# A macaron layer on one core: the recurrence's gates in two groups, the value products behind the transposes, the last sum of squares in its own tile

## The chip, the cores and the metric

The kernel runs on one core of one Trainium2 chip. The core's engines run side by side and each takes its own instructions in order: TensorE (PE, with its weight loader PEld), VectorE (DVE), ScalarE (ACT), GpSimd (POOL), and SyncE (SP), which issues transfers; ACT and POOL issue some too. An instruction that waits holds all that is queued behind it on its engine. The time of a kernel is the device time of one execution in microseconds (us).

## The reference

One layer, 512 tokens of width 1024 in float32: a half-step SwiGLU feed-forward (2816 wide), a mixer, and a second half-step feed-forward. Each is normed before and behind, and added to the stream.

```python
def hybrid_mixer(h, ...):
    proj = h @ w_in                     # x_lru, gate_lru, q, k, v
    y_lru = rg_lru(x_lru, ...) * jax.nn.gelu(gate_lru)
    y_attn = sliding_window_sink_attention(q, k, v, sinks)
    y = jnp.concatenate([rms_norm(y_lru, g_lru_out), rms_norm(y_attn, g_attn_out)], axis=-1)
    return y @ w_o

def rg_lru(x_in, ...):                  # 512 channels
    xc = causal_depthwise_conv(x_in, conv_w, conv_b)
    r = sigmoid(block_diag(xc, w_rg, b_rg))      # 8 blocks of 64x64
    i = sigmoid(block_diag(xc, w_ig, b_ig))
    log_a = LRU_C * r * log_sigmoid(lam)
    u = sqrt(-expm1(2.0 * log_a)) * (i * xc)
    return scan of h = exp(log_a) * h + u
```

The attention has 8 query heads of 64 in two groups, each group with one key and value head, windows of 128 tokens (a query block of 128 looks at its own block of keys and the one before), and a sink in the softmax. The very last step is the root mean square norm of the second feed-forward's output and the addition to the stream:

```python
def rms_norm(x, g):
    y = x * rsqrt(mean(x * x, axis=-1) + 1e-6)
    return y * g
```

## The kernel before, in words

All large products are made from two parts of each number: x = xh + xl, where `xh` is rounded to the short form (fp32r) that PE multiplies fast and `xl` is the rest. `mm3` (lines 500 to 507) issues hi·xh, hi·xl, lo·xh; these are the lines L505, L506 and L507 of every timeline. ACT makes the high part by a cast and POOL or DVE the low part by a subtraction. Weights are split likewise as they arrive (`whi_...` on ACT, `wlo_...` on DVE or POOL).

The order of the work is written out by hand: each engine works in the order in which the program calls it.

The mixer's stretch around the change goes so. The inner channels and tokens lie with the channels on the partitions: 512 channels are four chunks of 128 channels by 512 tokens. PE makes the products of k (`pk`), v (`pv`) and the four chunks of q (`pq0` to `pq3`), some 24 matmuls of 0.23 us each. Beside them DVE makes the causal convolution of chunks 0 and 1, and then of 2 and 3 (`conv`, L1442 to L1446), and scales each product from PSUM as it comes (`scaled`, L1426). `in_parts` (L1483 to L1493) does this for k and q, copies the first block to `home` and splits the rest in two parts.

`split_xc(ci)` (L1472, L1473) splits the convolution's output: the cast on ACT, the subtraction on POOL. `lru_gates(ci)` makes the two gates of a chunk: six matmuls with 64 rows each, the two halves of the partitions side by side (L1454), two sigmoids on ACT (L1456, L1458), two transfers on SP which bring the halves of both gates to where they belong (L1457, L1459), the multiplication of the input gate with the channels on POOL (L1461), and a third transfer which POOL issues (L1462). It is called for chunk j behind `pq`j. Behind `pq0` and its gates v is transposed (`vt`, L1512). SP also loads the weights of the mixer's output (`raw_wo`, L174), between these transfers.

The first query block has only its own keys; its scores (`cur`, L1610) are sixteen small products of 64 rows straight from `home`, for head 0 to head 3, and need all four chunks of q. They stand behind `pq3` and its gates.

Then come the attention's rounds (the loop over `now`). A unit is a query block and a group of heads, 8 units in all. In round `now` the scores of unit `now` are masked and their maxima taken on DVE, the exponentials are made on ACT (`exps`, L1652); unit `now`−1 is transposed on PE (`turn_p`, `pt`, L1664), copied out by ACT (L1666) and masked by POOL into `pp` and `pa` (L1670, L1671); and unit `now`−2 is multiplied with v (`values`, `po`, L1683 and L1684). Transposes and value products use plain float32. Between them `pump(n)` issues n steps of the gate's product (`gt`), each of three matmuls, so that PE has work. `PUMPS` gives how many go ahead of the transposes, and how many between them and the value products. In round 5 and 6 the recurrence's square roots stand on ACT (`root`, with two table loads).

The tail makes the last feed-forward's output in blocks of 128 tokens; the last block (`tb` = 3) comes in three pieces of 512, 256 and 256 columns. For each piece DVE takes the product out of PSUM (L1983), ACT squares and sums it (L1984) and DVE multiplies it with the gain (L1988). When all three sums are there, they are added on DVE (L1986, L1990), ACT takes the root (L1995), DVE the reciprocal (L1996), and three DVE operations multiply and add the stream (L1999); three transfers write them out (L2000).

Of the kernel before, what the change touches and what calls it, by code (L numbers as in the profile page):

```python
# [8 lines left out]
F32 = mybir.dt.float32  # L9
F32R = mybir.dt.float32r  # L10
U8 = mybir.dt.uint8
AF = mybir.ActivationFunctionType
ALU = mybir.AluOpType
AX = mybir.AxisListType

P = 128
T = 512
NB = T // P
D = 1024
# [4 lines left out]
KC = C // P  # L24
HD = 64
EPS = 1e-6
# [4 lines left out]
NWS = 6  # L31
NRAW = 5
CLASSIC1, CLASSIC2 = 4, 6
PUMPS = [(2, 1)] * 8 + [(1, 1), (1, 0), (4, 0)]
FILLS = {1: 4, 2: 5, 4: 5, 5: 5, 7: 5}
WARM = 6
AHEAD = 4
# [84 lines left out]
def tile_layer(ctx: ExitStack, tc: tile.TileContext, out: bass.AP, **ins: bass.AP):  # L122
    nc = tc.nc
    pe, dve, act, pool, sync = nc.tensor, nc.vector, nc.scalar, nc.gpsimd, nc.sync
# [5 lines left out]
    small = ctx.enter_context(tc.tile_pool(name="small", bufs=4))  # L130
# [8 lines left out]
    SIDE = [slice(0, HD), slice(HD, P)]  # L139

    def bank(name):
        return psum.tile([P, T], F32, tag="bank", name=name)

    def t2k(name, dt=F32):
        return big.tile([P, T], dt, tag="t2k", name=name, bufs=NT2K)
# [3 lines left out]
    def fours(name, dt):  # L149
        t = big.tile([P, NB * T], dt, tag="z", name=name, bufs=2)  # L150
        return [t[:, i * T:(i + 1) * T] for i in range(NB)]
# [10 lines left out]
    def wt(name, w=T, dt=F32):  # L162
        return tmp.tile([P, w], dt, tag="w", name=name, bufs=NW)
# [23 lines left out]
    class Shared:  # L187


        parts = slice(0, KD // 2), slice(KD // 2, KD)  # L190
# [259 lines left out]
    for name, n in ROWS:  # L450
        if name in ("b_rg", "b_ig"):

            j = name == "b_ig"
# [14 lines left out]
    def filled(name, w, value):  # L468
        t = const.tile([P, w], F32, name=name)
        dve.memset(t, value)  # L470
        return t
# [5 lines left out]
    eps4 = filled("eps4", 1, 4 * EPS)  # L477
    dummy = const.tile([P, 1], F32, name="dummy")

    def preload(func):  # L480
        act.activation(dummy, eps, func)
# [9 lines left out]
    def col(name, i):  # L491
        return colrange(name)[:, i:i + 1]
# [16 lines left out]
    def product(w, xs, sl=ALL, name="", hooks=()):  # L509
        ps = bank(name)  # L510
        hooks = dict(hooks)
        for k, x in enumerate(xs):
            if k in hooks:
                hooks[k]()
            mm3(ps[:, sl], w, k, [t[:, sl] for t in x], k == 0, k == len(xs) - 1)
        return ps
# [683 lines left out]
    banks = [bank(f"a_first{i}") for i in range(4)]  # L1200
# [96 lines left out]
    gw, home = {}, []  # L1297
# [60 lines left out]
    parts = [None] * KD  # L1358
# [63 lines left out]
    def in_product(name, hooks=(), ahead=AHEAD):  # L1422
        return product(W.take(ahead), mx.xs, name=name, hooks=hooks)

    def scaled(t, b):
        dve.tensor_mul(t, b, R)  # L1426
        return t
# [17 lines left out]
                ci = c0 + j  # L1445
                dve.scalar_tensor_tensor(xcs[ci], xps[ci][:, 1 + w:1 + w + T], col("conv_w", w * KC + ci), xcs[ci], op0=ALU.mult, op1=ALU.add)  # L1446

    def lru_gates(ci):

        banks = bank(f"rg{ci}"), bank(f"ig{ci}")  # L1450
        (hi, lo), (xh, xl) = gw["both"], xc_parts[ci]
        for i, (w, x) in enumerate(((hi, xh), (hi, xl), (lo, xh))):
            for ps, half in zip(banks, SIDE):
                pe.matmul(ps, w[half, ci, :], x[half, :], start=i == 0, stop=i == 2)  # L1454
        r, other, ig = t2k(f"r{ci}"), wt(f"other{ci}"), wt(f"ig{ci}")
        act.activation(r, banks[0], AF.Sigmoid, bias=col("b_rg", ci))  # L1456
        sync.dma_start(ig[SIDE[0], :], r[SIDE[1], :])  # L1457
        act.activation(other, banks[1], AF.Sigmoid, bias=col("b_ig", ci))  # L1458
        sync.dma_start(ig[SIDE[1], :], other[SIDE[0], :])  # L1459
        u = xcs[ci]  # L1460
        pool.tensor_mul(u, ig, u)  # L1461
        pool.dma_start(r[SIDE[1], :], other[SIDE[1], :])  # L1462
        t = t2k(f"th{ci}")
        rs_.append(r)
        us_.append(u)
        th.append(t)

    xc_parts = {}

    def split_xc(ci):  # L1470
        xh, xl = wt(f"xch{ci}", T, F32R), wt(f"xcl{ci}", T, F32R)
        act.copy(xh, xcs[ci])  # L1472
        pool.tensor_sub(xl, xcs[ci], xh.bitcast(F32))  # L1473
        xc_parts[ci] = xh, xl
# [8 lines left out]
    def in_parts(b, first, name, low=dve):  # L1483

        x = scaled(wt(name), b)
        dve.tensor_copy(first, x[:, :P])
        if name == "qT3":
            spare.extend(fours("attn", F32R))
            xh, xl = spare.pop(), spare.pop()
        else:  # L1490
            xh, xl = t2k(f"{name}h", F32R), t2k(f"{name}l", F32R)
        act.copy(xh, x)
        low.tensor_sub(xl, x, xh.bitcast(F32))  # L1493
        return xh, xl

    conv(0, xps)
    split_xc(0)
    kT = in_parts(pk, k0, "kT", pool)
    pv = in_product("pv")
    vT = scaled(wt("vT"), pv)  # L1500
    conv(2, xps)
    qT = []
    for j in range(4):
        b = in_product(f"pq{j}")
        if j < KC - 1:
            split_xc(j + 1)
        lru_gates(j)
        qT.append(in_parts(b, q0[:, j * P:(j + 1) * P], f"qT{j}", deferred if j == 3 else dve))
        if j == 0:
            vt = bank("vt")  # L1510
            for b in range(NB):
                pe.transpose(vt[:, b * P:(b + 1) * P], vT[:, b * P:(b + 1) * P], ident)  # L1512
            v = home[0][:, 3 * T:]
            dve.tensor_copy(v, vt)
# [50 lines left out]
    now = 0  # L1565
    steps = fill_steps()

    def pump(n):
        for _ in range(n):
            next(steps, None)  # L1570
# [12 lines left out]
    def root(ci):  # L1583
        act.activation(th[ci], th[ci], AF.Sqrt)
# [10 lines left out]
    scale = HD ** -0.5  # L1595
# [121 lines left out]
    for now in range(n_units + 2):  # L1717
        if now < n_units:
            scores(*units[now])
            if now in FILLS:  # L1720
                W.fill(FILLS[now])
        pump(PUMPS[now][0])
        if 0 <= now - 1 < n_units:
            turn_p(*units[now - 1])
        if now < n_units:
            exps(*units[now])
        if now == 0:
            deferred.run()
        if now <= n_units:
            run_due(now - 1)  # L1730
        pump(PUMPS[now][1])
        if 0 <= now - 2:
            values(*units[now - 2])
        if now == 5:
            for ci in range(KC):
                root(ci)
            preload(AF.Exp)
        if now == 6:
            for ci in range(KC):
                root_u(ci)  # L1740
            for ci in (2, 3):
                scan(ci)
        if now == n_units:
            scan(0)
            deferred.run()
            preload(AF.Sqrt)
            root_rms(slice(0, NB - 1))
# [62 lines left out]
    ws, banks = [], []  # L1810
    for c in range(EARLY):
# [9 lines left out]
        if c == EARLY - 2:  # L1821
            bcs = [l.spread() for l in lrms]
            for ci in range(KC):
                for h in range(2):
                    dve.tensor_mul(hl[ci][:, HALF[h]], hl[ci][:, HALF[h]], bcs[h])
                y = t2k(f"ylh{ci}", F32R), t2k(f"yll{ci}", F32R)
# [15 lines left out]
    banks = boundary(res, late, ysp, None, n2, "m")  # L1842
# [23 lines left out]
    parts = {(tb, dh): hbm.tile([P, T], F32, name=f"yp_b{tb}{dh}") for tb in range(NB) for dh in range(2)}  # L1866
# [43 lines left out]
    grow = []  # L1910

    def read_gain():
        for dh in range(2):
# [3 lines left out]
    last = {-1: [lambda: (read(0, 0), read(0, 1), read(1, 0), read(1, 1), read_gain(), read_x(0))],  # L1917
            2: [lambda: hid.fetched(f0, h_hbm[f0])], 3: [lambda: read_x(1)], 4: [lambda: (hid.split(f0), hid.split(f0 + 1))]}
# [42 lines left out]
    pieces = {tb: [(0, 0, T)] + ([(1, 0, T // 2), (1, T // 2, T)] if tb == NB - 1 else [(1, 0, T)]) for tb in range(NB)}  # L1961
# [13 lines left out]
    for tb in range(NB):  # L1975
        end = tb == NB - 1
        last = []
        ss = small.tile([P, 3], F32, tag="ss3", name=f"ss_b{tb}")
        tot = small.tile([P, 1], F32, tag="tot", name=f"tot_b{tb}")
        for i, (dh, c0, c1) in enumerate(pieces[tb]):  # L1980
            out_products(tb, i, range(f0 + 2 * ((tb, i) in started), f1))
            y = parts[tb, dh][:, c0:c1]
            dve.scalar_tensor_tensor(y, place(tb, i), -1.0 if dh else 1.0, y, op0=ALU.mult, op1=ALU.subtract if dh else ALU.add)  # L1983
            act.activation(wt(f"ysq{tb}{i}")[:, :c1 - c0], y, AF.Square, accum_out=ss[:, i:i + 1])  # L1984
            if end and i == 2:
                dve.tensor_add(tot, ss[:, 0:1], ss[:, 1:2])  # L1986
            last.append(wt(f"last{tb}{i}")[:, :c1 - c0])
            (dve if end or i else pool).tensor_mul(last[i], y, grow[dh][:, c0:c1])  # L1988
        if end:
            dve.tensor_add(tot, tot, ss[:, 2:3])  # L1990
        else:
            dve.tensor_add(tot, ss[:, 0:1], ss[:, 1:2])

        rs = small.tile([P, 1], F32, tag="rs1", name=f"rs_b{tb}")
        act.activation(rs, tot, AF.Sqrt, bias=eps4, scale=4.0 / D)  # L1995
        dve.reciprocal(rs, rs)  # L1996
        for i, (dh, c0, c1) in enumerate(pieces[tb]):
            y = parts[tb, dh][:, c0:c1]
            dve.scalar_tensor_tensor(y, last[i], rs, x_rows[tb][:, dh * T + c0:dh * T + c1], op0=ALU.mult, op1=ALU.add)  # L1999
            (act if end and i == 1 else sync).dma_start(out[0, tb * P:(tb + 1) * P, dh * T + c0:dh * T + c1], y)  # L2000
# [28 lines left out]
```

## Time and profile before

| | us |
|---|---|
| median of 3 runs | 845.67 (845.57 to 845.91) |
| span of the profiled execution | 843.6 |
| PE busy | 834.5 (99%) |
| DVE busy | 732.7 (87%) |
| ACT busy | 523.8 (62%) |
| POOL busy | 201.7 (24%) |

The profiled execution took 843.6 us from its first to its last instruction; what lies around that span is in the median and not in the profile. The mean granted clock of TensorE is 0.998.

A row of a timeline gives the start, the duration, the engine, the line, the operation, the tiles (out<-in), their shape, how many instructions stand in the row, and in brackets the idle time ahead of it on its engine with what ended it. Matmuls overlap in the pipeline: the distance between the starts of two is what one costs, not the duration. A row of the waits gives an engine's line and what it waited for: the sum in us, how often, and the longest.

### The profile page before, as it was taken

How to read it: one execution, taken by the hardware profiler on the slowest of the kernel's cores; microseconds unless marked ns; L12 is line 12 of the kernel's file. 1: busy time of each engine (PE TensorE's matmuls, PEld its weight loads, DVE VectorE, ACT ScalarE, POOL GpSimd, SP SyncE). 2: the span in 40 equal slices, each digit the busy share in tenths (PEclk: the TensorE clock that was granted, in tenths of full speed). 3: DMA queues.
4: the chain of work that ended last, by engine and by line, in shares of the span. 5: the costliest groups of instructions: out<-in, count | busy, mean ns of one | idle time of the engine just before them, and what ended most of it. 6: DMA issues, size and time to landing. Idle time of an engine off the chain costs nothing.

```text
span 843.6 us, 12618 instructions
## 1 busy us (share of the span) xinstructions
PE 834.5 (99%) x4568; PEld 722.6 (86%) x4568; DVE 732.7 (87%) x1020; ACT 523.8 (62%) x874; POOL 201.7 (24%) x214
## 2 busy tenths in 40 slices
PE   9999999999999999999999999999999999999996
PEld 8988888988988998997788899888888888888885
DVE  4978999998979865889899589799998998998996
ACT  6646856666666655456788457436757767666552
POOL 2023000140320333334646055112004113032001
PEclk9999999999999999999999999999999999999999
DMA  7249419397595799222511131169539939769742
GB/s 251 77 131 348 151 59 322 80 254 254 129 248 185 169 261 343 77 79 91 158 50 51 50 110 42 50 137 273 186 108 231 322 91 249 249 154 262 295 137 101
DMA packets 123615, 143.75 MB, mean 170 GB/s; under 512 B 23896, under 2 KB 81568, under 8 KB 123040
## 3 DMA queue, kind: packets, MB, share of 16 engines
q1 hardware_dynamic: 109232, 111.86, 41.6%
q0 software_dynamic: 14176, 30.94, 17.0%
q8 instruction: 36, 0.59, 0.3%
q14 instruction: 27, 0.22, 0.1%
q10 hardware_dynamic: 144, 0.13, 0.0%
HBM read 100.45 MB, written 40.89 MB: 168 GB/s over the span
## 4 chain that ended last, share of the span: by engine, by line
PE 97%; ACT 1%; DVE 1%; DMA 1%; issue 0%; POOL 0%; DVEq 0%; POOLq 0%; ACTq 0%
PE ab L955 10%; PE aa L955 10%; PE da L955 5%; PE db L955 5%; PE yaa L1345 3%; PE bb L955 3%; PE ba L955 3%; PE yda L1345 2%; PE ya L507 2%; PE ya L505 2%; PE ya L506 2%; PE a_first L1205 1%; PE aa L885 1%; PE yab L1875 1%; PE yab L1874 1%; PE yab L1876 1%
## 5 line engine op out<-in xcount | busy, mean ns | idle before, releaser
L1115 POOL DMA_DIRECT2D yp_a<-stage x42 | 36.9, 1085 | 181.2 <-ACT stage L1112 160.9
L1115 POOL DMA_DIRECT2D yp_b<-stage x42 | 36.4, 1091 | 144.6 <-ACT stage L1112 121.1
L505 PE MATMUL ya<-hha,whi_ad 128*128 128x512 f32 x62 | 24.1, 389 | 0.0
L506 PE MATMUL ya<-hla,whi_ad 128*128 128x512 f32 x62 | 24.1, 389 | 0.0
L507 PE MATMUL ya<-hha,wlo_ad 128*128 128x512 f32 x62 | 24.1, 389 | 0.0
L688 POOL TENSOR_TENSOR acca_r<-acca_r,sq_r 128x512 f32<-128x512 f32 x6 | 8.2, 1359 | 51.4 <-ACT sq_r L536 51.4
L1988 POOL TENSOR_TENSOR last<-yp,grow 128x512 f32<-128x512 f32 x3 | 3.9, 1290 | 57.7 <-DVE yp L1983 57.7
L524 PE MATMUL an<-xh_mx,whi_xl 128*128 128x256 f32 x64 | 15.8, 287 | 0.0
L1984 ACT ACTIVATE ysq<-yp 128x512 f32<-128x512 f32 (+1 forms) x9 | 5.3, 585 | 16.5 <-DVE yp L1983 16.0
L525 PE MATMUL an<-xh_mx,wlo_xl 128*128 128x256 f32 x64 | 15.5, 283 | 0.0
L505 PE MATMUL gt<-xh_mx,whi_gt 128*128 128x512 f32 x32 | 14.2, 444 | 0.0
L1112 ACT COPY stage<-yab 128x512 f32<-128x512 f32 x12 | 6.5, 604 | 11.7 <-DMA yp_b<-stage 7.4
L507 PEld LDWEIGHTS ya<-hha,wlo_ad 128*128 128x128 f32 x62 | 11.6, 188 | 2.4
L506 PEld LDWEIGHTS ya<-hla,whi_ad 128*128 128x128 f32 x62 | 11.6, 188 | 2.4
L505 PEld LDWEIGHTS ya<-hha,whi_ad 128*128 128x128 f32 x62 | 11.6, 188 | 2.4
L536 ACT ACTIVATE sq_r<-yp_a 128x256 f32<-128x256 f32 (+1 forms) x10 | 5.0, 502 | 12.9 <-DVE yp_a L678 5.9
L505 PE MATMUL pq<-xh_mx,whi_q 128*128 128x512 f32 x32 | 12.8, 400 | 0.0
L505 PE MATMUL pub<-xh_f,whi_bu 128*128 128x512 f32 x32 | 12.6, 395 | 0.0
L507 PE MATMUL gt<-xh_mx,wlo_gt 128*128 128x512 f32 x32 | 12.6, 394 | 0.0
L505 PE MATMUL pgb<-xh_f,whi_bg 128*128 128x512 f32 x32 | 12.6, 393 | 0.0
L506 PE MATMUL gt<-xl_mx,whi_gt 128*128 128x512 f32 x32 | 12.5, 392 | 0.0
L580 ACT ACTIVATE xh_f<-xT,cols 128x256 fp32r<-128x256 f32 x16 | 8.1, 509 | 7.0 <-DVE xT L719 6.4
(2014 smaller groups left out, 3535.0 us busy)
## 6 DMA issues: line engine op xcount, KB each, us to landing
yp_a<-stage POOLq DMA_DIRECT2D x50, 256.0 KB, 8.9
yp_b<-stage POOLq DMA_DIRECT2D x50, 256.0 KB, 9.2
h_a<-za SPq DMA_DIRECT2D x16, 256.0 KB
hxa<-h_a SPq DMA_DIRECT2D x16, 256.0 KB
h_b<-zb SPq DMA_DIRECT2D x16, 256.0 KB
hxb<-h_b SPq DMA_DIRECT2D x16, 256.0 KB
xn<-in_x SPq DMA_DIRECT2D x8, 256.0 KB
xT_hbm<-xT POOLq DMA_DIRECT2D x2, 1024.0 KB, 9.7
```

The costliest lines, as they stand in the source:

```text
L505: pe.matmul(ps, hi[:, k, :], xh, start=start, stop=False)
L506: pe.matmul(ps, hi[:, k, :], xl, start=False, stop=False)
L507: pe.matmul(ps, lo[:, k, :], xh, start=False, stop=stop)
L524: pe.matmul(ps[:, sl], hi[:, k, :], xh, start=k == 0, stop=False)
L525: pe.matmul(ps[:, sl], lo[:, k, :], xh, start=False, stop=False)
L885: pe.matmul(o, w[:, k, js], x, start=first and i + j + k == 0, stop=k == 3 and i == 2, skip_group_check=True)
L955: pe.matmul(b[tb], x[:, blk], w[:, k, :], start=first and q + k + j == 0, stop=q + k == 2 and j == 2, skip_group_check=True)
L1115: pool.dma_start(o, st.rearrange("p (a b) -> p a b", a=2) if len(o.shape) == 3 else st, accum_op=ALU.add)
L1205: pe.matmul(banks[j][:, HALF[0]], ws[j][part][:, k, :], n1.xs[k][xpart][:, HALF[0]], start=k == 0 and part == xpart, stop=stop and k == KD ...
L1345: pe.matmul(o, a[:, k, ms], x[:, js], start=first and i + k + m % 2 == 0, stop=k == 1 and i == 2, skip_group_check=True)
L1874: pe.matmul(banks[i], hh[:, js], hi[:, k, :], start=first and k == 0, stop=False, skip_group_check=True)
L1875: pe.matmul(banks[i], hh[:, js], lo[:, k, :], start=False, stop=False, skip_group_check=True)
```

## The change

Three parts, all in the mixer and the tail.

The gates: `lru_gates` takes a list of chunks. It is called behind `pq0` for chunks 0 and 1 and behind `pq2` for chunks 2 and 3, and issues for each of the three products the matmuls of both chunks, and after all twelve the sigmoids, transfers and multiplications of one chunk and then the other (now in `sigmoids`). `split_xc(1)` is called ahead of `pv`, `split_xc(2)` and `split_xc(3)` behind `pq1`.

The rounds: `PUMPS` has one number a round. All steps of the gate's product stand ahead of the transposes, and the value products directly behind the transposes.

The tail: the third piece's sum of squares has a tile of its own, `ss_last`. While it is made, DVE adds the first two sums, already scaled and with the epsilon, into `tot`; the root on ACT takes `ss_last` as its input and `tot` as its bias. The gain multiplications of the second and third piece stand behind the root's issue.

```diff
-PUMPS = [(2, 1)] * 8 + [(1, 1), (1, 0), (4, 0)]
+PUMPS = [3] * 8 + [2, 1, 4]
...
-    def lru_gates(ci):
-
-        banks = bank(f"rg{ci}"), bank(f"ig{ci}")
-        (hi, lo), (xh, xl) = gw["both"], xc_parts[ci]
-        for i, (w, x) in enumerate(((hi, xh), (hi, xl), (lo, xh))):
-            for ps, half in zip(banks, SIDE):
-                pe.matmul(ps, w[half, ci, :], x[half, :], start=i == 0, stop=i == 2)
+    def lru_gates(cs):
+
+        banks = {ci: (bank(f"rg{ci}"), bank(f"ig{ci}")) for ci in cs}
+        hi, lo = gw["both"]
+        for i in range(3):
+            for ci in cs:
+                xh, xl = xc_parts[ci]
+                w, x = ((hi, xh), (hi, xl), (lo, xh))[i]
+                for ps, half in zip(banks[ci], SIDE):
+                    pe.matmul(ps, w[half, ci, :], x[half, :], start=i == 0, stop=i == 2)
+        for ci in cs:
+            sigmoids(ci, banks[ci])
+
+    def sigmoids(ci, banks):
         r, other, ig = t2k(f"r{ci}"), wt(f"other{ci}"), wt(f"ig{ci}")
...
     split_xc(0)
     kT = in_parts(pk, k0, "kT", pool)
+    split_xc(1)
     pv = in_product("pv")
...
         b = in_product(f"pq{j}")
-        if j < KC - 1:
-            split_xc(j + 1)
-        lru_gates(j)
+        if j == 1:
+            split_xc(2)
+            split_xc(3)
+        if j in (0, 2):
+            lru_gates((j, j + 1))
         qT.append(in_parts(b, q0[:, j * P:(j + 1) * P], f"qT{j}", deferred if j == 3 else dve))
...
-        pump(PUMPS[now][0])
+        pump(PUMPS[now])
         if 0 <= now - 1 < n_units:
             turn_p(*units[now - 1])
...
-        pump(PUMPS[now][1])
         if 0 <= now - 2:
             values(*units[now - 2])
...
-            act.activation(wt(f"ysq{tb}{i}")[:, :c1 - c0], y, AF.Square, accum_out=ss[:, i:i + 1])
-            if end and i == 2:
-                dve.tensor_add(tot, ss[:, 0:1], ss[:, 1:2])
+            if i == 2:
+                ss_last = small.tile([P, 1], F32, tag="tot", name="ss_last")
+                act.activation(wt(f"ysq{tb}{i}")[:, :c1 - c0], y, AF.Square, accum_out=ss_last)
+                dve.tensor_scalar(tot, ss[:, 0:1], 4.0 / D, 4 * EPS, op0=ALU.mult, op1=ALU.add)
+                dve.scalar_tensor_tensor(tot, ss[:, 1:2], 4.0 / D, tot, op0=ALU.mult, op1=ALU.add)
+            else:
+                act.activation(wt(f"ysq{tb}{i}")[:, :c1 - c0], y, AF.Square, accum_out=ss[:, i:i + 1])
             last.append(wt(f"last{tb}{i}")[:, :c1 - c0])
-            (dve if end or i else pool).tensor_mul(last[i], y, grow[dh][:, c0:c1])
+            if not end or i == 0:
+                (dve if end or i else pool).tensor_mul(last[i], y, grow[dh][:, c0:c1])
+        rs = small.tile([P, 1], F32, tag="rs1", name=f"rs_b{tb}")
         if end:
-            dve.tensor_add(tot, tot, ss[:, 2:3])
+            act.activation(rs, ss_last, AF.Sqrt, bias=tot, scale=4.0 / D)
+            for i, (dh, c0, c1) in list(enumerate(pieces[tb]))[1:]:
+                dve.tensor_mul(last[i], parts[tb, dh][:, c0:c1], grow[dh][:, c0:c1])
         else:
             dve.tensor_add(tot, ss[:, 0:1], ss[:, 1:2])
-
-        rs = small.tile([P, 1], F32, tag="rs1", name=f"rs_b{tb}")
-        act.activation(rs, tot, AF.Sqrt, bias=eps4, scale=4.0 / D)
+            act.activation(rs, tot, AF.Sqrt, bias=eps4, scale=4.0 / D)
         dve.reciprocal(rs, rs)
```

## The prediction

> **What bounds the kernel now.** I read the page's head first, then the waits of TensorE (PE) and of its weight loader (PEld), then the timelines of the three stretches that the diff touches.
>
> ```profile
> span 843.6 us, 12618 instructions
> ...
> PE 834.5 (99%) x4568; PEld 722.6 (86%) x4568; DVE 732.7 (87%) x1020; ACT 523.8 (62%) x874; POOL 201.7 (24%) x214
> ```
> ```profile
> PE warm L1192 <- POOL ident masks.py:199: 1.4, 1, 1.4
> ...
> PE pt L1664 <- ACT sc L1652: 0.3, 1, 0.3
> ```
> ```profile
> 380.00:410.30 30.30, 30.30 (x154) 23.38 (x152) 26.59 (x33) 18.65 (x27) 16.98 (x12) 1.00 0.39 115
> ```
>
> PE is busy 99% of the span and waits 1.4 us at its start and else no longer than 0.3 at once (columns: sum, count, longest); the table by stretches (length, then busy time of PE, PEld, DVE, ACT, POOL) shows it busy for all 30.30 us of the stretch with the gates, at a granted clock of 1.00. So the time here is PE's, and only three kinds of thing can move it: steps between matmuls that are longer than they need be, matmuls that come to wait, and the last microseconds, where PE has stopped and a chain of DVE and ACT runs out. No matmul is added or removed. The profiled span is 843.6 us and the median of the runs 845.67, so 2.07 us lie around the span; I work out a difference on the span and add it to the median.
>
> **Gates: switches saved.** The gate products use half the rows (64*128), two side by side.
>
> ```profile
> 401.66 0.39 PE L507 MATMUL pq<-xh_mx,wlo_q 128*128 128x512 f32 x1
> 401.98 0.49 PE L1454 MATMUL rg<-xch,gates 64*128 64x512 f32 x1
> ...
> 402.31 0.39 PE L1454 MATMUL rg<-xcl,gates 64*128 64x512 f32 x1
> ...
> 402.54 0.39 PE L1454 MATMUL rg<-xch,gates 64*128 64x512 f32 x1
> ...
> 402.86 0.50 PE L505 MATMUL pq<-xh_mx,whi_q 128*128 128x512 f32 x1
> 403.20 0.40 PE L506 MATMUL pq<-xl_mx,whi_q 128*128 128x512 f32 x1
> ```
>
> An ordinary step is 0.23 (402.31 to 402.54). Into the block it is 0.32, its first step 0.33, out of it 0.32, and the first full one 0.34: 0.09 + 0.10 + 0.09 + 0.11 = 0.39 us that one isolated block of a chunk costs. Two groups instead of four blocks leave out the switches of chunk 1's block, −0.39. Chunk 3's block now follows chunk 2's, but `cur`, which used to follow chunk 3's block and has 64 rows too, now follows full matmuls of pq3, so that saving is paid back there: 0 (−0.05 at best).
>
> The row says that the price is per change of tile size. The Trainium skill, page "TensorEngine Tiling (Array Packing)", section Key Properties, has it as "Changing tiling mode (not just tile) drains the TensorE". By that rule too three entries go and one comes, the sum being the same, and the trace agrees with the 0.32 against 0.23.
>
> **Gates: what becomes late.** Chunk 1's and chunk 3's low parts `xcl` are now needed a whole pq (6.5 us) earlier. They are made on POOL.
>
> ```profile
> 385.89 1.31 POOL L1493 TENSOR_TENSOR kTl<-kT,kTh 128x512 fp32r<-128x512 f32 x1
> ...
> 396.66 1.31 POOL L1461 TENSOR_TENSOR xc<-ig,xc 128x512 f32<-128x512 f32 x1 [3.76 <-DMA ig<-other]
> 397.90 0.56 POOL L1462 DMA_DIRECT2D r<-other  x1
> 399.37 2.16 POOL L1473 TENSOR_TENSOR xcl<-xc,xch 128x512 fp32r<-128x512 f32 x1 [0.92 <-ACT xch L1472]
> 402.90 1.75 POOL L1461 TENSOR_TENSOR xc<-ig,xc 128x512 f32<-128x512 f32 x1 [1.36 <-DMA ig<-other]
> ...
> 405.15 1.30 POOL L1473 TENSOR_TENSOR xcl<-xc,xch 128x512 fp32r<-128x512 f32 x1
> 407.07 2.36 POOL L1461 TENSOR_TENSOR xc<-ig,xc 128x512 f32<-128x512 f32 x1 [0.63 <-DMA ig<-other]
> ```
> ```profile
> 386.75 1.52 DVE L214 TENSOR_TENSOR wlo_q<-raw_q,whi_q 128x1024 fp32r<-128x1024 f32 x1 [0.73 <-ACT whi_q L209]
> 388.20 0.68 DVE L1426 TENSOR_TENSOR vT<-pv,R_mx 128x512 f32<-128x512 f32 x1
> ...
> 399.17 1.21 DVE L214 TENSOR_TENSOR wlo_gt<-raw_gt__4051,whi_gt 128x1024 fp32r<-128x1024 f32 x1
> ```
>
> The same POOL operation takes 1.30 us or up to 2.36. The `xcl` of 2.16 us was issued 0.20 behind DVE's `wlo_gt` (399.17 to 400.38) and ended 1.15 behind that one's end: the two take turns. The five rows from 396.66 on exceed 1.30 by 0.01, 0.86, 0.45, 0 and 1.06, on the mean 0.47.
>
> The Trainium skill, page "SBUF — State Buffer", section "SBUF: two separate sides", calls DVE's and GpSimd's shared port pair "an exclusive lock, not a bandwidth split". It speaks against this change, which bunches POOL's work. With no lock the second stall below would by that rule be the 0.1 of its lower end; the 2.16 beside 1.30 agrees with the rule.
>
> First group: `xcl1` (1.3 us) stands on POOL ahead of `wlo_q`, from about 387.15. DVE's own `wlo_q` (386.75) comes 0.52 later since ACT casts `xch1` ahead of its input, meets the `xcl1` on POOL and ends at about 389.6 instead of 388.27. vT behind it then ends at 390.3.
>
> ```profile
> 389.33 0.66 PE L1512 MATMUL vt<-ident,vT 128*128 128x128 f32 x4
> ```
>
> PE wants vT for `vt` at 389.33 plus chunk 1's three steps of 0.23, some 390.0: a stall of 0.3, with the signal +0.33. With DVE not held it is 0; +0.35 is the upper end.
>
> Second group: PE enters the group at 401.98 − 0.39 + 0.33 = 401.92 and reaches `xcl3` three steps on (0.33 + 0.23 + 0.23), at 402.7. On POOL two multiplications and two DMA issues now stand ahead of `xcl2` and `xcl3`, with their inputs there just ahead of 396.66 (as before; I take 396.55) and about 1.2 later, 397.7 (chunk 1's two sigmoids stand directly behind chunk 0's on ACT). Never held off: 396.55 + 4 × 1.30 + 2 × 0.55 = 402.85, a stall of 0.1. Each held off by the mean 0.47: 404.75, a stall of 2.05. Laid against DVE's rows, shifted by the 0.45 that `wlo_q` and vT cost DVE, with each held where a DVE operation of SBUF runs: first multiplication to 398.15, second to 400.15, `xcl2` to 402.5, `xcl3` to 403.9. I take that, +1.15. The rotation DMAs on SP's queue pass ahead of the `raw_wo` load, which isn't needed in this stretch; I cost that at nothing: what hides it is pq2's six microseconds, and uncovered it would hold ACT's cast of `raw_wo`, not PE at once.
>
> `cur` at the end of the stretch:
>
> ```profile
> 408.63 0.69 DVE L1426 TENSOR_TENSOR qT<-pq,R_mx 128x512 f32<-128x512 f32 x1 [0.36 <-PE pq L507]
> 409.36 0.23 DVE L1486 COPY home<-qT 128x128 f32<-128x128 f32 x1
> ```
> ```profile
> 409.33 1.05 PE L1610 MATMUL cur<-home 64*128 64x128 f32 x16
> ```
>
> qT3's scaling and copy take 0.96 us (408.63 to 409.59) from the end of pq3's last matmul (0.39 long), and used to lie beside chunk 3's gate block (0.88, as 401.98 to 402.86) and the first twelve of cur's sixteen. Now cur begins directly behind pq3, and wants head 3 at 0.32 for the switch and 12/16 of its 1.05 less the overlap, some 1.07 us after pq3's last start; the copy is done 0.39 + 0.96 and two signals, some 1.45, after that start: +0.35. Lower end 0; upper 1.1, where POOL's multiplication of chunk 3 or 2 is running when the copy (SBUF to SBUF) comes.
>
> Sum for the gates: −0.39 + 0.33 + 1.15 + 0.35 = **+1.44** (from −0.4 to +3.1).
>
> **Attention rounds.** Each round keeps its gate-product steps; the transposes `pt` come one step later and the value products `po` stand right behind them.
>
> ```profile
> 413.85 0.74 PE L1664 MATMUL pt<-ident,sc 128*128 128x128 f32 x4
> ```
> ```profile
> 427.19 0.60 PE L1664 MATMUL pt<-ident,sc 128*128 128x128 f32 x4
> 427.54 0.48 PE L505 MATMUL gt<-xh_mx,whi_gt 128*128 128x512 f32 x1
> 427.86 0.39 PE L506 MATMUL gt<-xl_mx,whi_gt 128*128 128x512 f32 x1
> 428.09 0.40 PE L507 MATMUL gt<-xh_mx,wlo_gt 128*128 128x512 f32 x1
> 428.32 0.33 PE L1683 MATMUL po<-home,pp 128*128 128x64 f32 x2
> 428.49 0.39 PE L1684 MATMUL po<-home,pa 128*128 128x64 f32 x2
> ```
>
> The first full matmul behind the transposes takes 0.32 (427.54 to 427.86) instead of 0.23, which a merged round has once instead of twice: −0.09. The first po pair takes 0.17 beside 0.23 for the others, as its weights load under a full matmul, and loses this: +0.05. So −0.045 a round, and in the rounds without another wait (2 to 5) −0.18 (0 to −0.4). The very first pt (413.85) is 0.74 long instead of the 0.60 of the other, since its exponentials are just late; a step later it doesn't wait: −0.15.
>
> ```profile
> 442.41 1.38 PE L1664 MATMUL pt<-ident,sc 128*128 128x128 f32 x4 [0.28 <-ACT sc L1652]
> ```
> ```profile
> 442.06 1.43 POOL L1670 TENSOR_SCALAR_AFFINE_SELECT pp<-pa 128x512 f32<-128x512 f32 x1 [5.81 <-ACT pa L1666]
> 443.56 0.64 POOL L1671 TENSOR_SCALAR_AFFINE_SELECT pa<-pa 128x512 f32<-128x512 f32 x1
> ```
>
> Round 7's pt starts 0.28 late and is 1.38 long instead of 0.60: about 1.06 us of stall. I expect no gain there: pt a step later finds its operands, but the po right behind it needs POOL's two selections, done at 444.20, and PE would reach them at about 443.5. What is late next is the chain ACT copy, POOL selections, which itself starts from PE; so the stall changes its place. Were the chain early enough, up to −1.2. Sum: **−0.33**.
>
> **Tail.**
>
> ```profile
> 836.91 0.42 DVE L1983 SCALAR_TENSOR_TENSOR yp<-ybl,yp 128x256 f32<-128x256 f32 x1
> ...
> 837.70 0.42 ACT L1984 ACTIVATE ysq<-yp 128x256 f32<-128x256 f32 x1 [0.56 <-DVE tot_b L1986]
> ...
> 838.24 0.16 DVE L1990 TENSOR_TENSOR tot_b<-tot_b,ss_b 128x1 f32<-128x1 f32 x1 [0.45 <-ACT ysq L1984]
> 838.43 0.29 ACT L1995 ACTIVATE rs_b<-tot_b,eps 128x1 f32<-128x1 f32 x1 [0.23 <-DVE tot_b L1990]
> 838.76 0.16 DVE L1996 RECIPROCAL rs_b<-rs_b 128x1 f32<-128x1 f32 x1 [0.36 <-ACT rs_b L1995]
> ```
>
> The last Square waits for `tot_b` although its own input is done earlier (−0.1 to −0.28, as its tile is now its own); DVE's addition between Square and Sqrt goes (−0.2); the multiplication that held DVE until 836.91 moves behind the sum, which can then start at 836.70 (−0.2). Sqrt and reciprocal follow 0.6 earlier: **−0.6**. Lower gain −0.3, if DVE's two moved multiplications (0.42 each) delay the reciprocal; upper −0.7.
>
> Sum: 1.44 − 0.33 − 0.6 = **+0.5 us**.
>
> **The rivals.** (a) POOL is in time: its four operations run unheld and `xcl3` stalls 0.1. Then −0.39 + 0.33 + 0.1 + 0.35 − 0.33 − 0.6 = −0.5: 845.1. For it: three of the POOL rows show at most 0.45 of delay. Against: DVE has 26.59 of 30.30 us busy there. (b) All that can be gained is gained, round 7's stall too: −0.4 − 1.5 − 0.7 = −2.6: 843.1. Against it: the POOL wait of 5.81 us on ACT's copy. (c) The other side: POOL and DVE take turns at the price of the upper ends, in the second group (2.05) and at the copy before `cur` (1.1): 3.1 − 0.33 − 0.6 = +2.2: 847.9. It decides from stalls of about 2.6 us together. For it: 2.36 and 2.16 in the rows. (d) The grouping doesn't do what it says, each chunk's pair paying its own switch: the −0.39 goes, 846.6. Against: within a block pairs with other weights follow at 0.23.
>
> **How the numbers follow.** 0.2% of 845.67 is 1.7 us, about what can be told from no change. Forecast 0.47, (a) 0.15, (b) 0.12, (c) 0.21, (d) 0.05. The likeliest gives 845.67 + 0.5 = 846.2, its own range 845.2 to 847.2. Faster by over 0.2% only (b) and some of (a)'s upper ends: 0.16. Slower only (c): 0.23. The range 843.4 to 848.1 leaves out parts of (b) and (c).
>
> **What would show it.** Steps of 0.23 between chunk 0's and chunk 1's gate products and one entry fewer; a gap ahead of `vt`; PE idle inside the second group, released by POOL's `xcl`; gaps inside `cur`, released by DVE's copy; po right behind pt and the stall near 443 us released by POOL instead of ACT; the last reciprocal 0.6 earlier after the last matmul. I am wrong if POOL's rows in the second group stay near 1.3 us, or round 7's stall vanishes.

## The result and the profile after

The changed kernel takes 848.94 us (median of 5, 848.42 to 849.41) against 845.67 of the kernel before (844.72 to 846.19 in all): the ratio is 1.0036, with a 95% interval of 1.0025 to 1.0047. So it is slower by some 3.3 us; 846.2 was forecast, and the range ended at 848.1.

The head of the page after, and its waits of PE (sum, count, longest):

```profile
span 847.7 us, 12616 instructions
...
PE 834.3 (98%) x4568; PEld 722.6 (85%) x4568; DVE 736.9 (87%) x1020; ACT 524.1 (62%) x874; POOL 200.2 (24%) x214
```
```profile
PE cur L1620 <- DVE home L1493: 1.7, 1, 1.7
...
PE rg L1457 <- POOL xcl L1480: 0.9, 1, 0.9
PE po L1694 <- POOL pa L1681: 0.7, 2, 0.4
PE xtp L1139 <- DMA xn<-in_x: 0.7, 2, 0.4
PE ab L955 <- ACT bb L960: 0.6, 1, 0.6
PE sc L1631 <- ACT sc L1662: 0.3, 1, 0.3
```

PE's work is the same (834.3 against 834.5 us); the span is longer by waits. `cur`, `rg`, `po` and `sc` lie in the changed stretches. `xtp` and `ab` don't: they are waits of the first and of the second feed-forward that the profile before doesn't have and that differ from kernel to kernel below, and I have no cause for them.

PE's timeline of the second gate group and of `cur`:

```profile
402.81 0.39 PE L1457 MATMUL rg<-xcl,gates 64*128 64x512 f32 x1
...
404.15 0.49 PE L1457 MATMUL rg<-xcl,gates 64*128 64x512 f32 x1 [0.94 <-POOL xcl L1480]
...
410.73 0.94 PE L1620 MATMUL cur<-home 64*128 64x128 f32 x12
413.33 0.49 PE L1620 MATMUL cur<-home 64*128 64x128 f32 x4 [1.66 <-DVE home L1493]
413.75 0.50 PE L505 MATMUL gt<-xh_mx,whi_gt 128*128 128x512 f32 x1
```

The step from chunk 2's to chunk 3's low part is 1.34 instead of 0.23, and `cur` takes 3.02 us (410.73 to 413.75) where it took 0.98. From the first matmul of `pq0` to the first of `gt` it is 30.34 us (383.41 to 413.75), before 27.41 (382.90 to 410.31): +2.93, which is the 1.11, the 2.04 and 0.18 at `vt` (0.51 behind the last gate matmul instead of 0.33), less 0.39 for the switches. From there to the transposes of the attention's output it is 46.04 against 45.81 (they start at 459.79, before at 456.12): +0.23. The tail is 0.72 shorter, as shown below. That makes +2.44, and the span of this profile, the slowest of the five executions, is 4.1 us longer. The other 1.66 lie outside the changed work: 0.51 ahead of `pq0`, 0.79 between those transposes and the last matmul, 0.36 behind the last reciprocal. Such stretches scatter between the profiles (`pq0` starts at 382.43 to 383.41 in the kernels of this document), so of the 3.3 us by the medians some 2.4 have a place and the rest has none.

Why the two waits stand there is seen on POOL and on DVE (after), and on the same DVE operation before:

```profile
397.19 1.30 POOL L1468 TENSOR_TENSOR xc<-ig,xc 128x512 f32<-128x512 f32 x1 [4.86 <-DMA ig<-other]
398.42 0.56 POOL L1469 DMA_DIRECT2D r<-other  x1
398.99 1.31 POOL L1468 TENSOR_TENSOR xc<-ig,xc 128x512 f32<-128x512 f32 x1
400.24 0.54 POOL L1469 DMA_DIRECT2D r<-other  x1
400.80 1.30 POOL L1480 TENSOR_TENSOR xcl<-xc,xch 128x512 fp32r<-128x512 f32 x1
402.82 1.27 POOL L1480 TENSOR_TENSOR xcl<-xc,xch 128x512 fp32r<-128x512 f32 x1 [0.73 <-DVE qT0l L1500]
```
```profile
398.61 4.05 DVE L1500 TENSOR_TENSOR qT0l<-qT,qT0h 128x512 fp32r<-128x512 f32 x1
...
410.24 0.69 DVE L1500 TENSOR_TENSOR qT2l<-qT,qT2h 128x512 fp32r<-128x512 f32 x1 [1.09 <-ACT qT2h L1499]
410.85 1.22 DVE L214 TENSOR_TENSOR wlo_gt<-raw_gt__4103,whi_gt 128x1024 fp32r<-128x1024 f32 x1
411.98 0.68 DVE L1426 TENSOR_TENSOR qT<-pq,R_mx 128x512 f32<-128x512 f32 x1
412.70 0.57 DVE L1493 COPY home<-qT 128x128 f32<-128x128 f32 x1
```
```profile
397.97 0.68 DVE L1493 TENSOR_TENSOR qT0l<-qT,qT0h 128x512 fp32r<-128x512 f32 x1
```

None of these POOL operations is held: each takes 1.3 us. It is DVE that is held. Its `qT0l`, an operation of 0.68 before, begins at 398.61, in POOL's first transfer issue, and takes 4.05 us: it ends 0.56 behind the last of what follows without a gap on POOL, the second multiplication, the second issue and the subtraction of chunk 2. The low part of chunk 3 lies in the buffer that qT0 had and must wait for that very operation (the 0.73 in its row). DVE is then 3.4 us behind; and ahead of `qT2l` stand the four sigmoids on ACT, which now come together, so that DVE comes to qT3 only at 411.98, 1.2 us after PE has ended its product (its last matmul starts at 410.41 and is 0.39 long).

### The profile page after: what moved, and what is told of

It is laid out like the page before. It is cut to its first block, busy times and chain, and to the rows that moved or that the text cites. A ratio compares the mean times of both kernels' runs of the same rounds, so it can differ in the third digit from the quotient of the medians.

```text
span 847.7 us, 12616 instructions
## 1 busy us (share of the span) xinstructions
PE 834.3 (98%) x4568; PEld 722.6 (85%) x4568; DVE 736.9 (87%) x1020; ACT 524.1 (62%) x874; POOL 200.2 (24%) x214
## 4 chain that ended last, share of the span: by engine, by line
PE 89%; DVE 5%; issue 2%; ACT 2%; POOL 1%; DMA 1%; SPq 0%; DVEq 0%; ACTq 0%; POOLq 0%
PE aa L955 10%; PE ab L955 10%; PE da L955 5%; PE db L955 4%; PE yaa L1345 3%; PE bb L955 3%; PE ba L955 3%; PE yda L1345 2%; PE ya L507 2%; PE ya L506 2%; PE ya L505 2%; PE aa L885 1%; PE a_first L1205 1%; PE yab L1883 1%; PE yab L1885 1%
## 5 line engine op out<-in xcount | busy, mean ns | idle before, releaser
L507 PE MATMUL pq<-xh_mx,wlo_q 128*128 128x512 f32 x32 | 12.5, 390 | 0.0
```

Of the source, the lines that this page charges most:

```text
L507: pe.matmul(ps, lo[:, k, :], xh, start=False, stop=stop)
```

## The experiments

The kernel before ran beside each set; its medians were 845.48 (24 runs), 845.30 (22), 845.75 (15) and 845.50 (15). Differences are against the one of the same set. Between two changed kernels a difference of under some 1.4 us is inside what the intervals leave open.

**The three parts alone.** Each kernel is the one before with the hunks of one part of the diff.

> Only the gates part of the change. Theory A (the loss is the gates' alone: the wait for the low part of chunk 3 and the wait inside cur, both because POOL's operations run back to back and hold DVE): PE waits 0.9 us at the gates' matmul for xcl and 1.7 us inside cur for home, as in the changed kernel, and the time is 2.5 to 3.2 us over before. Rival B (part of the loss comes from the three parts together): under 1.5 us over before.

Measured: 849.72, +4.24 (ratio 1.0049, 1.0036 to 1.0061), with the same two waits (1.7 and 0.9). So by the medians the gates' part alone costs more than the whole change. What its profile has beside the two waits is seen in the timeline behind `cur`, and in the table by stretches, whose third number from the end is the granted clock:

```profile
414.86 0.63 PE L507 MATMUL gt<-xh_mx,wlo_gt 128*128 128x512 f32 x1
415.29 0.63 PE L505 MATMUL gt<-xh_mx,whi_gt 128*128 128x512 f32 x1
```
```profile
413.00:414.00 1.00, 1.00 (x7) 0.79 (x8) 0.56 (x1) 1.00 (x1) 0.99 (x2) 1.00 1.06 372
...
415.00:416.00 1.00, 1.00 (x4) 0.81 (x3) 0.93 (x3) 0.00 (x0) 0.05 (x1) 0.50 1.08 376
```

About 1.3 us after the wait inside `cur` (it ends at 412.92) the clock falls to a half for some 3.4 us, and the matmuls step by 0.43 instead of 0.23: 1.6 us. This isn't in every execution: two of the five have a mean clock of 0.999 and take 849.06 and 849.72, on the mean 0.45 less than the other three. Where it isn't, part of the 1.6 is lost all the same, by an estimate from this trace some 0.7: the first exponentials start at 416.17 and end at about 417.6, when unslowed transposes would stand ready at 413.34 + 3.54 = 416.88 (3.54 is their distance from `gt` before).

> Only the rounds part. Theory A: the merged rounds save 0.045 us each and the waits of rounds 4, 7 and 8 in the changed kernel come from the rounds themselves: between -0.3 and +0.3 us. Rival B: those waits come from DVE and ACT being late behind the gates; alone, this part gains 0.8 us or more. Rival C: the transposes one step later cost more than they save wherever ACT and POOL are the bound: +0.5 us or more.

Measured: 846.52, +1.04 (1.0013, 1.0004 to 1.0022): rival C. The trace gives half of it a place: the wait of round 4, 0.58 us where before it hardly stalled. The scores of block 2, and on ACT the copy of the second transposes and the exponentials that the scores wait for, with the two ACT rows before:

```profile
425.02 0.38 PE L1621 MATMUL sc<-kTh,qT2h 64*128 64x256 f32 x1 [0.58 <-ACT sc L1652]
```
```profile
419.50 0.58 ACT L1666 COPY pa<-pt 128x512 f32<-128x512 f32 x1
...
424.17 0.37 ACT L1652 ACTIVATE sc<-sc,nm 128x128 f32<-128x128 f32 x1 [0.75 <-DVE nm L1641]
```
```profile
419.26 0.58 ACT L1666 COPY pa<-pt 128x512 f32<-128x512 f32 x1
...
423.93 0.37 ACT L1652 ACTIVATE sc<-sc,nm 128x128 f32<-128x128 f32 x1 [0.75 <-DVE nm L1641]
```

These exponentials begin 41.56 us after `pq0`'s first matmul (382.61), before 41.03 (382.90); PE comes to the scores 0.18 earlier. The copy of the second transposes is as late, 36.89 against 36.36, and so is that of the first, 32.60 against 32.06: the delay is there from the first transposes on and is handed down ACT's queue.

> Only the tail part. In the changed kernel the reciprocal starts 1.65 us after the last matmul's start, before 2.37: so -0.7 us by the theory that nothing behind it takes this back. Rival: the output transfers end at the same time, since they wait for others ahead of them: 0.

Measured: 844.77, −0.71 (0.9993, 0.9984 to 1.0002; 11 runs). The size is the one that was expected, though the interval alone doesn't exclude zero. The last matmul and the reciprocal of the changed kernel:

```profile
840.85 0.28 PE L1861 MATMUL ybl<-whi_br,hlb 128*128 128x256 f32 x1
...
842.50 0.16 DVE L2011 RECIPROCAL rs_b<-rs_b 128x1 f32<-128x1 f32 x1
```

The reciprocal comes 1.65 us behind the start of the last matmul, before 2.37 (836.39 to 838.76).

**One group only.**

```diff
-        if j < KC - 1:
+        if j in (1, 2):
             split_xc(j + 1)
-        lru_gates(j)
+        if j != 1:
+            lru_gates((0, 1) if j == 0 else (j,))
```

> Only chunks 0 and 1 in one group; chunks 2 and 3 each behind its own q product as before. Theory A: POOL then has no four operations back to back (POOL's second multiplication stands behind the subtraction of chunk 2 only if ACT is in time), DVE isn't held for microseconds, cur waits for nothing; -0.39 for the switch and up to +0.35 at vt: between -0.4 and 0. Rival: the bunching of the first two chunks' multiplications already holds DVE, and cur or the gates of chunk 2 wait: +0.5 us or more.

Measured: 847.76, +2.28 (1.0014 to 1.0034): the rival. Five of the eight executions have a mean clock of 0.998 or 0.999 and take 846.53 to 847.93, the three at 0.996 or 0.997 take 848.19 to 848.36, so it holds without the half clock too. The first group is enough to put POOL's row together:

```profile
PE cur L1619 <- DVE home L1493: 2.0, 1, 2.0
```
```profile
397.69 4.06 DVE L1500 TENSOR_TENSOR qT0l<-qT,qT0h 128x512 fp32r<-128x512 f32 x1
```

**The suspected cost taken away.** The changed kernel, with

```diff
-        pool.tensor_mul(u, ig, u)
+        if ci > 1:
+            pool.tensor_mul(u, ig, u)
```

> The changed kernel without POOL's two multiplications of chunks 0 and 1 by the input gate; the recurrence of these chunks is then computed from ungated channels. Theory A (these two, the transfer issues and the two subtractions run back to back on POOL and keep DVE's qT0l out for 4 us; everything late on DVE follows from it): qT0l takes 0.7 to 2 us instead of 4.05, the wait for chunk 3's low part goes (-1.1), the wait inside cur falls below 0.6 us (-1.3 or more): 2.2 to 2.8 us under the changed kernel. Rival B (cur waits because ACT makes four sigmoids ahead of qT2's high part): only the gates' wait goes, cur's stays over 1.2 us: about 1.1 us under.

Measured: 845.86, +0.56 of before (0.9997 to 1.0014), so 2.7 us under the changed kernel: theory A, inside its bounds. The waits, and the operation on DVE that was held:

```profile
PE rg L1457 <- POOL xcl L1481: 0.3, 1, 0.3
...
PE cur L1621 <- DVE home L1494: 0.2, 1, 0.2
```
```profile
398.11 0.69 DVE L1501 TENSOR_TENSOR qT0l<-qT,qT0h 128x512 fp32r<-128x512 f32 x1 [0.42 <-ACT qT0h L1500]
```

**The sigmoids behind qT2's parts.**

```diff
+        if j == 2:
+            for ci in (2, 3):
+                sigmoids(ci, gate_banks[ci])
```

(behind the line that appends to `qT`, instead of at the end of `lru_gates`.)

> The changed kernel with the sigmoids of chunks 2 and 3 behind the parts of qT2 on ACT; all else is the same. Theory A: qT2's scaling on DVE is itself late (408.20), so qT2h is ready only at about 409.4 instead of 410.2 and cur's wait falls by no more than 0.8 us. Rival B: the four sigmoids are what qT2h, DVE's weight subtraction and qT3 stand behind; cur's wait falls under 0.6 us, 1.3 us or more under the changed kernel.

Measured: 848.12, +2.82. The waits:

```profile
PE sc L1636 <- ACT sc L1667: 1.1, 1, 1.1
...
PE cur L1625 <- DVE home L1492: 0.7, 1, 0.7
```

The wait inside `cur` falls from 1.7 to 0.7, by a little more than theory A allowed and less than rival B asked, so the sigmoids carry some 1.0 of it; but the wait of the scores in round 4 rises from 0.3 to 1.1 and takes back most. The median is 0.45 under the changed kernel's, which the intervals don't separate.

**The multiplications behind the subtractions.** `sigmoids` keeps POOL's two calls back, and they are made after `split_xc(3)`.

> The changed kernel with POOL's multiplications of chunks 0 and 1, and their transfer issues, behind the subtractions of chunks 2 and 3. Theory A: the low part of chunk 3 is in time (-1.1); qT0l isn't held, but DVE's next subtraction of two SBUF inputs, wlo_gt, meets the same chain of four POOL operations and is held instead: cur's wait stays between 0.6 and 1.7 us; in sum 1 to 2 us under the changed kernel. Rival: the chain of operations isn't what holds DVE but only its first two; then cur doesn't wait and the time is 2.5 us under.

Measured: 852.69, +7.39 (1.0069 to 1.0094). Neither: it is the slowest of all.

```profile
PE cur L1630 <- DVE home L1500: 4.7, 1, 4.7
```
```profile
404.03 0.69 DVE L1426 TENSOR_TENSOR qT<-pq,R_mx 128x512 f32<-128x512 f32 x1 [3.66 <-POOL xc L1478]
```

qT1's scaling takes the buffer of chunk 0's input gate, which the multiplication must have read before. I had reckoned POOL's row and left out who waits for its buffers.

**The rounds from the fourth on.**

```diff
-PUMPS = [(2, 1)] * 8 + [(1, 1), (1, 0), (4, 0)]
+PUMPS = [(2, 1)] * 4 + [(3, 0)] * 4 + [(2, 0), (1, 0), (4, 0)]
```

> The kernel before, with the value products behind the transposes only from round 4 on; rounds 0 to 3 as before. My theory of the rounds part (the transposes of rounds 1 to 3, a step later, hold up ACT, whose queue makes the exponentials and the weight casts behind the copy of the transposes; the scores of round 4 then wait for banks that the exponentials free): the wait of round 4 is gone, and the time lies between -0.4 and +0.2 us of before. Rival: the loss is made in rounds 6 to 8, by the value products that wait for POOL's selections: +0.6 us or more over before.

Measured: 845.47, +0.17 (0.9991 to 1.0009). So the merged rounds are neither a gain nor a loss from round 4 on, the wait of round 4 isn't in the trace, and by difference the loss of the rounds' part lies in rounds 0 to 3.

**Another buffer, another queue.** The changed kernel with chunk 3's low part in a buffer of another pool, and, separately, with the issues of chunks 0 and 1 on SP:

```diff
-        pool.dma_start(r[SIDE[1], :], other[SIDE[1], :])
+        (sync if ci < 2 else pool).dma_start(r[SIDE[1], :], other[SIDE[1], :])
```

> The changed kernel with the low part of chunk 3 in a buffer of another pool, so that it needn't wait until DVE's qT0l has read its own. Theory A (POOL's row of operations holds DVE): POOL makes it directly behind chunk 2's, about 0.7 us earlier, and the gates' wait falls from 0.9 to about 0.3 us; but qT0l is held 1.3 us longer (5.3 instead of 4.05), and cur's wait grows by about as much. In sum -0.5 to +0.8 us of the changed kernel. Rival B (the buffer's wait is the cause of the second group's delay and of what follows): 1 us or more under the changed kernel.

Measured: 849.74, +3.99, 0.7 over the changed kernel: theory A. The wait of the gates goes and comes back inside `cur`:

```profile
PE cur L1621 <- DVE home L1494: 2.9, 1, 2.9
...
PE rg L1457 <- POOL xcl L1481: 0.2, 1, 0.2
```
```profile
397.92 5.29 DVE L1501 TENSOR_TENSOR qT0l<-qT,qT0h 128x512 fp32r<-128x512 f32 x1
```
```profile
400.11 2.54 POOL L1481 TENSOR_TENSOR xcl<-xc,xch 128x512 fp32r<-128x512 f32 x2
```

The time itself says less: this profile has the half clock behind `cur` too, and the two executions with a mean clock of 0.999 take 848.40 and 848.44, under the changed kernel's 848.94.

> The changed kernel with the two transfers r<-other of chunks 0 and 1 issued by SP instead of POOL. Theory A: POOL's row becomes 1.1 us shorter at most, since the second multiplication waits for its transfers; qT0l is held 2.9 to 3.6 us instead of 4.05, both waits of PE fall a little: 0.5 to 1.5 us under the changed kernel. Rival: it is these issues between the multiplications that shut DVE out; without them qT0l is held no longer than one POOL operation (under 2 us), and the time is 2 us or more under.

Measured: 850.25, +4.50, 1.2 over: both wrong on the time. `qT0l` takes 0.69, as the rival had it, and now POOL is the one that waits:

```profile
397.62 0.69 DVE L1500 TENSOR_TENSOR qT0l<-qT,qT0h 128x512 fp32r<-128x512 f32 x1
...
401.33 1.67 DVE L1500 TENSOR_TENSOR qT1l<-qT,qT1h 128x512 fp32r<-128x512 f32 x1
```
```profile
396.19 1.29 POOL L1468 TENSOR_TENSOR xc<-ig,xc 128x512 f32<-128x512 f32 x1 [4.85 <-DMA ig<-other]
399.07 2.13 POOL L1468 TENSOR_TENSOR xc<-ig,xc 128x512 f32<-128x512 f32 x1 [1.60 <-DVE home L1524]
401.16 2.96 POOL L1480 TENSOR_TENSOR xcl<-xc,xch 128x512 fp32r<-128x512 f32 x2
```

That it is the issues which shut DVE out isn't shown by this. POOL was idle when `qT0l` ran (397.48 to 399.07), and that idle time has a cause of its own: the moved issue stands on SP ahead of chunk 1's two transfers, so these are issued 2.29 us behind chunk 0's instead of 0.69. The second multiplication starts 1.91 us behind the end of the last of these issues, as the first does 1.92 behind the end of its own; DVE's copy, which its row names, makes none of its operands. Two POOL operations side by side with no issue between them are the subtractions. Here DVE's `qT1l`, waiting from 401.33, got in between them: the second ends later for it, both together take 2.96. With the own buffer, above, they take 2.54 and `qT0l` was kept out through both. What lets DVE in stays open.

The gates then wait 1.7 in two places for POOL, and `cur` still 1.3.

**Towards a faster version.** The gates' part and the tail, with

```diff
-        pool.tensor_mul(u, ig, u)
+        if ci < 2:
+            igs.append((u, ig))
+        else:
+            pool.tensor_mul(u, ig, u)
...
+        if j in (1, 2):
+            u, ig = igs[j - 1]
+            dve.tensor_mul(u, ig, u)
```

> Gates in two groups and the new tail, rounds as before; the multiplications of chunks 0 and 1 by the input gate on DVE, ahead of qT1's and qT2's scaling. Theory A: with no row of operations on POOL, qT0l takes 0.7 us, the gates' wait is below 0.4 us and cur's below 0.5; the saved switches (0.39) and vt's wait (0.2) about cancel with these, and the tail's 0.7 us is left: -0.9 to 0 us of before. Rival: DVE, now with 1.3 us more to do, is late for cur by itself: +0.5 us or more.

Measured: 847.70, +1.95 (1.0017 to 1.0034), over the whole range that theory A gave. qT0l does take 0.69, but `cur` waits 1.6 us for a copy that is held until POOL's multiplication of chunk 3 is through:

```profile
410.76 1.28 POOL L1473 TENSOR_TENSOR xc<-ig,xc 128x512 f32<-128x512 f32 x1
```
```profile
410.51 1.62 DVE L1498 COPY home<-qT 128x128 f32<-128x128 f32 x1
```

The last kernel moves the multiplications of chunks 2 and 3 behind the first sum of exponentials (round 0) and the sigmoids of chunks 2 and 3 behind qT2's parts.

> The last kernel (gates in two groups, multiplications of chunks 0 and 1 on DVE, new tail, rounds as before) with POOL's multiplications of chunks 2 and 3 and their transfer issues only behind the first exponentials' sum, and the sigmoids of chunks 2 and 3 behind qT2's parts on ACT. If the rest of cur's wait comes from these multiplications, which hold the copy of qT3 on DVE (1.62 instead of 0.23 us in the last kernel), the copy takes 0.23 us, cur waits under 0.5 us and the time is 1.2 to 2 us under the last kernel's: 845.7 to 846.5, with the gates' wait of 0.7 us left. Rival: DVE is late for cur by its own work; cur still waits over 1 us.

Measured: 846.81, +1.31 (1.0009 to 1.0027), 0.6 under the last, less than expected, and the intervals overlap. The waits and the copy are as expected:

```profile
PE rg L1457 <- POOL xcl L1484: 0.8, 1, 0.8
PE sc L1644 <- ACT sc L1675: 0.5, 1, 0.5
...
PE cur L1633 <- DVE home L1497: 0.2, 1, 0.2
```
```profile
410.69 0.23 DVE L1497 COPY home<-qT 128x128 f32<-128x128 f32 x1
```

What is left is a wait of the gates for chunk 3's low part, which fell to 0.2 or 0.3 only where `cur` waited longer or multiplications were left out, and one of the scores behind the multiplications that went to round 0. No version with grouped gates beats the kernel before; the fastest measured is the kernel before with the new tail alone, 844.77.

## Why the prediction was wrong

The forecast of no clear change fell. The side on which it fell is rival (c)'s, DVE and POOL in each other's way, at more than its price of +2.2; but (c) had POOL held in the second group and DVE held at the copy before `cur`, and of the two only the second was seen, with 0.34 us (the copy takes 0.57 instead of 0.23).

- **Switches saved, −0.39:** nothing contradicts it. In the first group the steps between the chunks' products are 0.23 as forecast, and the sum of +2.93 closes with it. (The lower end of the gates' sum adds up to −0.3, not −0.4.)
- **`vt`, +0.33:** measured 0.18, by the mechanism named.
- **Second group, +1.15 (0.1 to 2.05):** measured 1.11, and yet the step is wrong. I had POOL's operations held off by DVE, and said I was wrong if POOL's rows stay near 1.3 us; they did. The size came from the buffer of qT0 and from DVE's 4.05 us, which is the opposite side of the same exchange. A right number from a wrong path, by luck.
- **`cur`, +0.35 (0 to 1.1):** the step that failed; measured 2.04. I took qT3's scaling to start when its product is done, as it did before (0.36 idle on DVE). It started 1.2 us later, since DVE itself was behind: 3.4 us by qT0l and, to some 1.0, the four sigmoids ahead of qT2h on ACT. I had followed DVE's delays into POOL and not back into DVE.
- **Rounds, −0.33:** wrong in sign; +1.04 alone, +0.23 in the trace of the whole. The −0.15 of the first transposes came out; the saving per merged round is some 0.02 instead of 0.045 (from the first `gt` step of one round to that of the next 3.42 against 3.44 us with the rounds alone), and the first `po` pair keeps its 0.17. What I left out is that the transposes one step later hold what stands behind their copy on ACT's queue: exponentials, casts, and by DVE's weight subtraction and maxima the exponentials of unit 3, which free the banks that round 4's scores wait for: 0.53 us late at each of these, in the trace of the rounds alone. That rounds 4 to 8 gain nothing, since the stall there changes its place, came out (the `po` waits of 0.7 for POOL in the table; 845.47 for the rounds from 4 on).
- **Tail, −0.6:** measured −0.72 in the trace and −0.71 in the medians.
- **The parts don't add up:** 4.24 + 1.04 − 0.71 = 4.57, the whole is 3.3. The intervals of the four medians leave room for the 1.3 between. In the profiles it is the stretch from `gt` to the transposes of the attention's output that differs: +1.17 with the gates alone, +0.49 with the rounds alone, +0.23 in the whole. Two readings are left. The profile of the gates alone has the half clock there, and that of the whole doesn't. And the first transposes one step later (the rounds' part) are no longer ahead of the exponentials that the gates' part makes late. Both are argued from the traces, and neither was tried by itself.

On the exchange between DVE and POOL: the row has DVE's operation shut out for 3.4 of its 4.05 us, through a multiplication and a subtraction on POOL and the transfer issues ahead of them. The Trainium skill, page "SBUF — State Buffer", section "SBUF: two separate sides", lets whichever starts first keep the port pair for the whole instruction. The trace agrees that one of the two is shut out altogether, but it is kept out for a row of instructions, longer than that sentence says.

## What to carry to other kernels

Where DVE and POOL are together busy for longer than the stretch lasts (here 26.6 and 17.0 of 30.3 us), moving a POOL operation is a change on both engines: lay both queues out in order, with the buffers that each instruction frees, and follow a delay until it comes back to the engine it began on. A transfer issue of half a microsecond between two POOL operations did not let DVE in (changed kernel, 398.61 on); whether DVE gets in between operations without one, the runs leave open. And what is moved one step later delays not its own consumer alone but all that stands behind it in that consumer's queue.

## What was not expected of the hardware

A wait of PE inside `cur` went in five profiles with a stretch at half clock (steps of 0.43 instead of 0.23): in the gates' part alone after 1.70 us, with one group after 2.02, with the own buffer after 2.9, with the multiplications on DVE after 1.62, each time for about 3.4 us; with the multiplications behind the subtractions it begins some 3.2 us into the wait of 4.7 and lasts about 6.8; not in the changed kernel's profile, after 1.66. So a short wait can cost twice, and not in every run. The Trainium skill, page "TensorE: Matmul & The Clock Gate", section "Why this matters for your kernels", asks for no idle gaps over about 3 us between matmuls; here 1.6 was enough once, and the measurement decides.
